# One decoder step on one core: bank matmuls issued singly, two side jobs re-timed, and the end of the program in another order

## The chip, the core and the metric

The kernel runs on one core of one Trainium2 chip. The metric is the device time of one execution in microseconds (us). The program is a single launch.

## What is computed

One inference step of a small two-layer decoder in float32, width 2048, on 1024 prompt positions and 8 single sample positions:

```
x  <- LayerNorm(ALPHA*x + (pool(x@w_in)[u] @ w_grp * scale * silu(gate)) @ w_out)   # layer A: causal pooling
k, v = shared_kv(x)                                                                # 4 heads of 64, partial rotary
x  <- LayerNorm(ALPHA*x + (attention_window128(q, k, v, sinks) * silu(gate)) @ w_out)  # layer B
LayerNorm: mean and variance over the 2048 channels, LN_EPS = 1e-5, gain g, offset b
```

Outputs are y for both kinds of positions and the new pool, key and value states.

## The kernel before

**Data and tiles.** Activations lie channel first: 128 channels on the partitions, positions along the free dimension. The positions are worked on in two chunks, c = 0 with 512 and c = 1 with 520 columns, of which a product takes half: 256 or 260. A float32 product is made of three float32r matmuls, high x high, high x low and low x high (lines 662, 663, 664), where "high" is a rounded copy (ScalarE, L491 for weights, L797 for activations) and "low" the rest (VectorE, L506 and L806).

**Seven products for eight.** Outside two plain stretches, a 2x2 block of a matrix product is made by seven products in Strassen's manner (`seven`). One of the seven, a *product* in this text, is a tile of weights with 8 x 3 = 24 matmuls into one PSUM bank. Sums of weight blocks and of activation blocks stand in DRAM for this. The banks of one block are called a, b and c. Bank b begins as the negated bank a, written there by ScalarE in `p0` (L603), and matmuls then add to it. Evictions are called p0 to p6; p6 copies the last bank (L635), p3 and p4 are subtractions on VectorE (L623, L628). An eviction is put off: it is issued at the start of the next product (`flush`, called by `begin`).

**Banks.** `psD` hands out a ring of three banks, `psW` four more where they are not used for attention scores (else the same ring), `psO` one. [...] 

**Phases.** ai (input product, pooling, gate), ao (output product) for both chunks, then bi (queries, gates, attention) and bo (output product) for both. In the order of time: ai0, ai1 (from 383 us), ao0, ao1 (from 910), bi0 plain (1075 to 1222), bi0 by sevens, bi1 (from 1508), bo0, bo1 (from 2117).

**The order of the work.** Each engine works through its instructions in the order of the source. That order comes from counters: `self.i` counts products (in the plain stretches half units), `at(n, go)` puts work n products later, and generators in `side` go on by one step at a time when `int(i / every)` changes and enough buffers are free. Two such jobs matter here:
- `sum_gen("wob")` makes the sums of the output projection's weight blocks, in 24 pieces: two loads of half a piece on SP, four adds on VectorE, a store on POOL. Pieces are begun while `on` is set, one at a time, three to four counts each. In bi0 it was set from count 4 to 24, and again in bi1 from count 8. The trace has five pieces in bi0 (1093 to 1149 us) and 19 in bi1 (1559 to 1875 us).
- `ln_gen(0, ...)` in the last phase bo1 is the first chunk's last LayerNorm: statistics, then for each of 8 pairs of tiles a load, a subtraction (L1027) and a product (L1030) on VectorE, two scalings on ScalarE (L1019) and a store.

Weights are loaded some seven products ahead on SP, split three to four ahead. A buffer is one of 54 slots; the one that was freed longest ago is taken next.

**The end** (`phase_end`). The last three blocks x, y, z = 5, 6, 7 are made in an order written out by hand (`TAIL`), and a table `steps` hangs work on each product. The second chunk's LayerNorm comes in two halves: columns 260 to 519 (Bh) get statistics early and are finished by `affine1` (two VectorE passes, L1434 and L1435) and `affine2` (two ScalarE passes, L1442, and a store). For the columns 0 to 259 (A) the statistics come after the last product: `sums_a` adds up by matmuls with a constant matrix `jr` (L1492), `moments` makes mean and reciprocal deviation in small steps between ScalarE and VectorE (L1508 to L1518, L1505), `turn` transposes the gain-scaled tiles (`scale`, L1454) on TensorE (L1537), `factors` transposes the deviation (L1526), `last_rows` adds mean and offset by matmuls (L1545), and `evict` multiplies and stores the rows (L1562 on ScalarE, L1557 on VectorE). `spare` copies the last four columns on POOL (L1457), `square` is L1403, `add` L1406 and L1407, `rest` L1398.

Of the kernel before, what the change touches and what calls it, by code (L numbers as in the profile page):

```python
# [16 lines left out]
P = 128  # L17
# [165 lines left out]
class Kern:  # L183
    def __init__(self, ctx, tc, io):
        self.tc, self.io = tc, io
        self.nc = tc.nc
        pool = lambda name, **kw: ctx.enter_context(tc.tile_pool(name=name, **kw))
        one = pool("one", bufs=1)
        self.smp = pool("smp", bufs=2)
        dram = pool("dram", bufs=1, space=bass.MemoryType.DRAM)  # L190
        self.psd = [pool(f"psd{i}", bufs=1, space=bass.MemoryType.PSUM) for i in range(3)]
        self.pso = pool("pso", bufs=1, space=bass.MemoryType.PSUM)
        self.four = None
        ctx.callback(self.use_four, None)
        self.prm = one.tile([P, N_PRM], F32, name="prm")
        self.cst = one.tile([P, N_CST], F32, name="cst")
        self.mki = one.tile([P, 64], U8, name="mki")
        self.jr = one.tile([P, P], F32R, name="jr")
        area = one.tile([P, NK * NST], F32, name="area")
        three = lambda a, b, c: area[:, a : a + b * c].rearrange("p (b c) -> p b c", b=b)  # L200
        self.carry = three(0, NK, NST)
        self.kdec, self.qd, self.sgd = three(0, 2, NDEC), three(16, NDEC, 8), three(80, 8, NDEC)
        self.flag = one.tile([P, 1], F32, name="flag")
        self.mem = Mem(pool("mem", bufs=1), NSLOT)
        self.n = 0
        self.i = self.e = self.lastO = self.turns = self.ring = 0
        self.posts, self.events, self.side = [], {}, []
        self.extra, self.on = None, False
        self.fresh = False
        self.ahead = 7, 4, 3  # L210
        dr = lambda n, s: dram.tile(s, F32, tag=n, name=n)
        self.Td, self.act, self.l_sq, self.l_sh = {}, {}, {}, {}
        for c, (_, T) in enumerate(CHUNKS):
            for n, k in (("x", "ai"), ("g", "ao"), ("h", "bi"), ("o", "bo")):
                if (k, c) in STRASSEN:
                    self.Td[n, c] = dr(f"t{n}{c}", [P, 8, 4, T // 2])
            self.act["x", c] = io[f"x{c}"]
            for n in ("g", "h", "o", "p"):
                self.act[n, c] = dr(f"{n}{c}", [P, NK, T])
        self.gbd = dram.tile([32, 2 * P], F32, tag="gbd", name="gbd")  # L220
        self.ws = {
            n: [dr(f"s{n}{q}", [P, 4, 1024]) for q in range(np_)]
            for n, np_ in (("wia", 16), ("woa", 8), ("wkv", 2), ("wib", 16), ("wob", 8))
        }
# [361 lines left out]
    def seven(self, c, z0, z1, after, c11=None, split=False, own=None):  # L586
# [13 lines left out]

        def p0():
            B["b"] = self.psD()
            nc.scalar.mul(B["b"][:, :TH], B["a"][:, :TH], -1.0)  # L603
            if split:
                nc.scalar.copy(out(0)[:, :TH], B["a"][:, :TH])
# [34 lines left out]
        def run(idx):  # L640
            bank = names[idx]
            w = self.begin()
            xs = [self.x_get((idx, g)) for g in range(2)]
            if self.fresh:

                self.fresh = False
                h = xs[0][0].rv(4, TH)[:, 0, :]
                for _ in range(3):
                    ps = self.psD()
                    nc.tensor.matmul(ps[:, :TH], w[0].r[:, :P], h, start=True, stop=True)  # L650
            new = bank not in B
            if new and own is not None and bank in "ac":
                B[bank] = own() if bank == "a" else B["a"]
            elif new:
                B[bank] = self.psW() if bank in "ac" else self.psD()
            ps = B[bank]
            wh, wl = (s.r for s in w)
            for k in range(8):
                s = slice(k * P, (k + 1) * P)
                h, l = (a.rv(4, TH)[:, k % 4, :] for a in xs[k // 4])  # L660
                on = not new
                nc.tensor.matmul(ps[:, :TH], wh[:, s], h, start=new and k == 0, stop=False, skip_group_check=on)  # L662
                nc.tensor.matmul(ps[:, :TH], wh[:, s], l, start=False, stop=False, skip_group_check=on)  # L663
                nc.tensor.matmul(ps[:, :TH], wl[:, s], h, start=False, stop=k == 7, skip_group_check=on)  # L664
            for s in w:
                s.free()
            for g in range(2):
                self.x_used((idx, g))
            self.posts.append(posts[idx])
            if idx in after:  # L670
                self.posts.append(after[idx])
            self.end()
# [695 lines left out]
    def phase_end(self, c, xs, x_in, pre, acc, gc, bc, out):  # L1368
# [116 lines left out]
        def sums_a(js):  # L1485

            z = SPLIT[-1]
            if not js:
                R[0] = self.psW(), self.psW()
            for ps, a, w in zip(R[0], (av, qv), (tv(z), self.pair_view(q[z], T))):  # L1490
                for j in js or (0, 1):
                    nc.tensor.matmul(  # L1492
                        ps[:, :TH], J, (w if js else a)[:, j, A], start=not js and j == 0, stop=js == (1,),
                        skip_group_check=True,
                    )

        def moments():

            mb, vb = R[0]
            w, h, S = self.mem.full(), self.mem.full(), [self.mem.half() for _ in range(4)]  # L1500
            m, v, qq, r = (t.a[:, :TH] for t in S)
            X, M = w.a[:, : 2 * P], h.r[:, : 2 * P]
            box["m"], box["r"], box["M"] = m, r, M
            hi, lo = slice(0, 64), slice(64, P)
            back32 = lambda k: nc.vector.tensor_sub(  # L1505
                M[k : k + 32], X[k : k + 32], h.a[k : k + 32, : 2 * P]
            )
            nc.scalar.copy(m, mb[:, :TH])  # L1508
            nc.vector.tensor_mul(qq, m, m)
            nc.scalar.mul(X[hi], mb[hi, A2], -1.0)  # L1510
            nc.vector.scalar_tensor_tensor(v, vb[:, :TH], EPS, qq, op0=ALU.add, op1=ALU.subtract)
            nc.scalar.activation(r, v, AF.Abs_reciprocal_sqrt)
            nc.scalar.copy(M[hi], X[hi])
            nc.vector.tensor_mul(qq, r, r)
            nc.vector.scalar_tensor_tensor(qq, qq, -0.5, v, op0=ALU.mult, op1=ALU.mult)
            nc.vector.scalar_tensor_tensor(r, qq, 1.5, r, op0=ALU.add, op1=ALU.mult)
            nc.vector.tensor_mul(X[lo], v[lo, A2], r[lo, A2])
            nc.scalar.copy(M[lo], X[lo])  # L1518
            back32(32)
            back32(96)  # L1520

        def factors():
# [53 lines left out]
        for p in SPLIT:  # L1576
            box, z0, z1 = self.two(T)

            def open_(p=p, box=box, z0=z0):
# [28 lines left out]
            (y, 6): [  # L1608
                lambda: add(x, A), lambda: rest(z, A), lambda: affine(y, Bh), lambda: spare(x), lambda: scale(x),
            ],  # L1610
            (z, 5): [lambda: square(y, A), lambda: affine(z, Bh), lambda: spare(4), lambda: scale(4)],
            (z, 6): [
                lambda: square(z, A, 0), lambda: add(y, A), lambda: scale(z, (0,), True),
            ],
        }
        for p, idx in TAIL:
            for go in steps.get((p, idx), []):
# [8 lines left out]
        while self.side:  # L1626
            self.side_step()
        self.flush()
        square(z, A, 1)
        spare(y)  # L1630
        spare(z)
        scale(z, (1,))
        scale(y)
        affine1(1, Bh)
        affine2(1, Bh)
        X[0, 0], X[0, 1] = self.psD(), self.psD()
        turn(0, 0, 8)
        sums_a(())
        sums_a((0,))
        sums_a((1,))  # L1640
        X[0, 2], X[0, 3] = self.psW(), self.psW()
        turn(0, 8, 16)
        X[1, 0], X[1, 1] = self.psO(), self.psD()
        turn(1, 0, 8)
        affine1(2, Bh)
        moments()
        X[1, 2] = self.psW()
        turn(1, 8, 12)
        affine2(2, Bh)
        box["c"] = self.psW()  # L1650
        factors()
        factors2()
        affine1(3, Bh)
# [5 lines left out]
        X[1, 3] = self.psD()  # L1659
        turn(1, 12, 16)  # L1660
        last_rows(1, (3,))
        affine2(3, Bh)
        affine1(4, Bh)
        for k in range(4):
            evict(1, k)
        affine2(4, Bh)
# [593 lines left out]
    def run(self):  # L2260
# [15 lines left out]
        for n, (kind, c, part) in enumerate(PHASES):  # L2276
            self.c, self.ph = c, kind + str(c)
            self.strassen = (kind, c, part) not in PLAIN
            self.shared = False
            self.fresh = c == 1 and before and self.strassen  # L2280
            before = c == 0 and self.strassen
            nxt = n + 1 if n + 1 < len(PHASES) else None
            self.every, self.room = 3, SIDE_KEEP
# [29 lines left out]
            elif (kind, c) == ("bi", 0) and not self.strassen:  # L2313
                self.summed["wob"] = 0
                self.extra = self.sum_gen("wob")
                for k in (4, 24):
                    self.at(k, lambda k=k: setattr(self, "on", k == 4))
                add(("h", 1, False), self.ln_gen(1, *acc[1], C_GA, C_BA, self.act["h", 1], self.Td.get(("h", 1))))
                for k in range(20):
                    self.at(2 * k + 3, lambda: self.side and self.lastO < self.i - 1 and self.side_step())  # L2320
# [9 lines left out]
                self.rt.free()  # L2330
            elif (kind, c) == ("bo", 1):
                gen = self.ln_gen(0, *acc[0], C_GB, C_BB, io["y0"], None)
                self.at(12, lambda gen=gen: add("y", gen))
                self.every = 1.6
            if kind == "ai":
                self.phase_ai(c, range(*part), nxt)
            elif kind == "bi":
# [155 lines left out]
```

## Time and profile before

| what | us |
|---|---|
| median of 3 runs | 2311.03 (2309.96 to 2313.41) |
| profiled execution, its own time | 2310.14 |
| its span, first to last instruction | 2308.4 |
| TensorE busy | 2283.8 |
| VectorE busy | 1905.4 |
| ScalarE busy | 1366.1 |

The span is what the profiler saw of one execution; 1.7 us of that execution's time lie around it. Engines are called PE (TensorE matmuls), PEld (its weight loads), DVE (VectorE), ACT (ScalarE), POOL and SP. A row of the timeline has the start in us from the span's start, the duration, engine, line, operation, written tile <- read tiles, shapes and count; in brackets stands how long the engine was idle before it and who ended that. Matmuls are pipelined, so the distance of two starts is what one costs, not its duration. A row "A <- B: t, n, m" of the waits says that A waited t us in n places for B, at most m in one.

### The profile page before, as it was taken

To read this page: it belongs to the slowest core of one execution; us is meant where nothing else is said; L and a number is where in the kernel's file an instruction comes from. 1 tells how busy PE (TensorE), PEld (TensorE's weight loads), DVE (VectorE), ACT (ScalarE), POOL (GpSimd) and SP (SyncE) were. 2 spreads that over 40 slices of the span, in tenths; PEclk is the share of its full clock that TensorE was granted. 3 is DMA by queue.
4 is the path that set the end of the run, shared out by engine and by line. 5 is a ranking of instruction groups with operands and counts; after the bars stand their busy time and mean duration, and the time that the engine had idled before them with its cause. 6 is when DMAs were issued, how large, how long until landed. Compare 5 with 4: busy or idle time off the path is not lost.

```text
span 2308.4 us, 50361 instructions
## 1 busy us (share of the span) xinstructions
PE 2283.8 (99%) x20258; PEld 2208.1 (96%) x20258; DVE 1905.4 (83%) x2434; ACT 1366.1 (59%) x2534; POOL 196.0 (8%) x396
## 2 busy tenths in 40 slices
PE   9999999999999999999999999999999999999997
PEld 7899999999999999999889999999999999999997
DVE  8787899777878878988978888899776777898897
ACT  4444445544546546555466776785777678646556
POOL 0111110010000000000101111100000000000001
PEclk9999999999999999999999999999999999999999
DMA  8668789988989988999777777787686768799785
GB/s 292 244 233 293 262 297 367 337 298 293 308 304 316 353 282 306 327 387 358 263 263 247 239 229 252 257 288 233 221 262 220 225 224 310 254 361 371 259 311 198
DMA packets 247978, 654.56 MB, mean 284 GB/s; under 512 B 25376, under 2 KB 106048, under 8 KB 247744
## 3 DMA queue, kind: packets, MB, share of 16 engines
q1 hardware_dynamic: 204576, 494.67, 63.8%
q0 software_dynamic: 43168, 156.68, 17.6%
q8 instruction: 158, 2.59, 0.5%
q14 instruction: 76, 0.62, 0.1%
HBM read 464.54 MB, written 177.20 MB: 278 GB/s over the span
## 4 chain that ended last, share of the span: by engine, by line
PE 53%; DVE 3%; issue 2%; DMA 1%; ACT 1%; POOL 0%; DVEq 0%; SPq 0%; POOLq 0%; ACTq 0%
PE pD L662 14%; PE pD L663 14%; PE pD L664 14%; PE pD L690 2%; PE pD L692 2%; PE pD L691 2%; PE pS L1823 2%; PE pS L1891 1%; PE pO L1930 1%; DMA m<-in_wob 1%; PE pD L1930 1%; PE pS L1930 1%; DMA m<-in_woa 0%; DVE m L506 0%; PE pO L662 0%
## 5 line engine op out<-in xcount | busy, mean ns | idle before, releaser
L662 PE MATMUL pD<-m,m 128*128 128x260 f32 (+1 forms) x4976 | 1409.1, 283 | 5.5 <-DVE m L623 2.2
L664 PE MATMUL pD<-m,m 128*128 128x260 f32 (+1 forms) x4976 | 1401.5, 282 | 0.1
L663 PE MATMUL pD<-m,m 128*128 128x260 f32 (+1 forms) x4976 | 1401.5, 282 | 0.0
L662 PEld LDWEIGHTS pD<-m,m 128*128 128x128 f32 x4976 | 936.9, 188 | 10.4 <-ACT pD L603 2.2
L664 PEld LDWEIGHTS pD<-m,m 128*128 128x128 f32 x4976 | 937.3, 188 | 0.3 <-DVE m L506 0.3
L663 PEld LDWEIGHTS pD<-m,m 128*128 128x128 f32 x4976 | 936.9, 188 | 0.5
L506 DVE TENSOR_TENSOR m<-m,m 128x1024 fp32r<-128x1024 f32 x684 | 827.8, 1219 | 77.2 <-ACT m L491 41.0
L491 ACT CAST m<-m 128x1024 fp32r<-128x1024 f32 x684 | 712.4, 1048 | 283.6 <-DVE m L343 86.8
L343 DVE TENSOR_TENSOR m<-m,m 128x1024 f32<-128x1024 f32 x120 | 146.6, 1222 | 10.0 <-DMA m<-in_wia 7.6
L806 DVE TENSOR_TENSOR m<-m,m 128x1024 fp32r<-128x1024 f32 (+1 forms) x118 | 144.2, 1225 | 7.6 <-ACT m L797 4.9
L635 ACT COPY m<-pD 128x260 f32<-128x260 f32 (+1 forms) x87 | 32.5, 374 | 191.5 <-PE pD L664 191.5
L797 ACT CAST m<-m 128x1024 fp32r<-128x1024 f32 (+1 forms) x118 | 123.6, 1052 | 4.3 <-DMA m<-in_x 2.5
L690 PE MATMUL pD<-m,m 128*128 128x512 f32 x288 | 114.3, 397 | 0.0
L692 PE MATMUL pD<-m,m 128*128 128x512 f32 x288 | 113.5, 394 | 0.0
L691 PE MATMUL pD<-m,m 128*128 128x512 f32 x288 | 113.3, 393 | 0.0
L623 DVE TENSOR_TENSOR m<-pD,m 128x260 f32<-128x260 f32 (+1 forms) x90 | 38.1, 423 | 74.7 <-PE pD L664 74.7
L1864 ACT ACTIVATE m<-m,sm 128x128 f32<-128x128 f32 x256 | 99.2, 390 | 0.0
L1886 ACT ACTIVATE m<-m,sm 128x128 f32<-128x128 f32 (+1 forms) x320 | 93.7, 372 | 0.0
L1134 PE MATMUL pD<-m,m 128*128 128x260 f32 (+1 forms) x528 | 91.4, 323 | 0.0
L1134 PEld LDWEIGHTS pD<-m,m 128*128 128x128 f32 x528 | 79.4, 188 | 8.2
L612 ACT COPY m<-pD 128x260 f32<-128x260 f32 (+1 forms) x90 | 33.7, 374 | 90.0 <-PE pD L664 89.7
L603 ACT ACTIVATE pD<-pD 128x260 f32<-128x260 f32 (+1 forms) x88 | 32.4, 369 | 81.6 <-PE pD L664 81.2
(258 smaller groups left out, 2183.8 us busy)
## 6 DMA issues: line engine op xcount, KB each, us to landing
m<-in_wib SPq DMA_DIRECT2D x132, 512.0 KB
m<-in_wia SPq DMA_DIRECT2D x122, 512.0 KB
swia<-m POOLq DMA_DIRECT2D x64, 512.0 KB, 4.9
m<-swia SPq DMA_DIRECT2D x64, 512.0 KB
m<-swoa SPq DMA_DIRECT2D x64, 512.0 KB
m<-swob SPq DMA_DIRECT2D x56, 512.0 KB
m<-in_wob SPq DMA_DIRECT2D x52, 512.0 KB
m<-in_woa SPq DMA_DIRECT2D x48, 512.0 KB
```

Of the source, the lines that this page charges most:

```text
L343: self.nc.vector.tensor_add(s[out].a[:, :1024], s[x].a[:, :1024], s[y].a[:, :1024])
L491: self.nc.scalar.copy(hi.r[:, :1024], self.stream[self.cast].src().a[:, :1024])
L506: self.nc.vector.tensor_sub(lo.r[:, :1024], s.src().a[:, :1024], hi.a[:, :1024])
L662: nc.tensor.matmul(ps[:, :TH], wh[:, s], h, start=new and k == 0, stop=False, skip_group_check=on)
L663: nc.tensor.matmul(ps[:, :TH], wh[:, s], l, start=False, stop=False, skip_group_check=on)
L664: nc.tensor.matmul(ps[:, :TH], wl[:, s], h, start=False, stop=k == 7, skip_group_check=on)
L690: nc.tensor.matmul(ps[:], wh[:, s], h, start=par == 0 and k == 0, stop=False)
L691: nc.tensor.matmul(ps[:], wh[:, s], l, start=False, stop=False)
L692: nc.tensor.matmul(ps[:], wl[:, s], h, start=False, stop=par == 1 and k == 7)
L797: self.nc.scalar.copy(h.r[:, :n], s.a[:, :n])
L806: self.nc.vector.tensor_sub(l.r[:, :n], s.a[:, :n], h.a[:, :n])
L1134: nc.tensor.matmul(ps[:, : cs.stop - cs.start], ws[:, s], d[:, cs], start=f0 and k == 0, stop=l0 and k == 3,)
```

## The change

Bank matmuls: the three at the start of a phase go; in their place `p0` issues one for each ring bank, the first time that the phase takes it as bank b, with the constant `jr` as weights and a resident activation tile as data. Weight sums: `on` is set from count 20 to 38 of bi0 instead of 4 to 24. Norm: the side job of bo1 starts at product 11 instead of 12 and goes on every 1.25 instead of 1.6 products. End: y's and z's work on `steps` is moved, all of z's statistics squares come in one, the sums come directly after them, `affine(z)` comes after the last product, `affine1(2)` and `affine2(1)` come after `moments`, `affine2(2)` behind the first evictions. In `moments` the negated mean is made from the copy in SBUF instead of from PSUM, and two small steps are exchanged. Five matmuls of 512 columns go into the bank of the factors ahead of them; nothing reads what they write.

```diff
-        self.fresh = False
+        self.fresh = None
...
         def p0():
             B["b"] = self.psD()
+            if self.fresh is not None and self.ring not in self.fresh:
+                self.fresh.add(self.ring)
+                nc.tensor.matmul(
+                    B["b"][:, :TH], self.jr[:], self.X[0, 0][0].rv(4, TH)[:, 0, :], start=True, stop=True
+                )
             nc.scalar.mul(B["b"][:, :TH], B["a"][:, :TH], -1.0)
...
-            if self.fresh:
-                self.fresh = False
-                h = xs[0][0].rv(4, TH)[:, 0, :]
-                for _ in range(3):
-                    ps = self.psD()
-                    nc.tensor.matmul(ps[:, :TH], w[0].r[:, :P], h, start=True, stop=True)
...
             nc.vector.tensor_mul(qq, m, m)
-            nc.scalar.mul(X[hi], mb[hi, A2], -1.0)
             nc.vector.scalar_tensor_tensor(v, vb[:, :TH], EPS, qq, op0=ALU.add, op1=ALU.subtract)
+            nc.scalar.mul(X[hi], m[hi, A2], -1.0)
+            nc.scalar.copy(M[hi], X[hi])
             nc.scalar.activation(r, v, AF.Abs_reciprocal_sqrt)
-            nc.scalar.copy(M[hi], X[hi])
+            back32(32)
...
             nc.scalar.copy(M[lo], X[lo])
-            back32(32)
             back32(96)
...
-            (z, 5): [lambda: square(y, A), lambda: affine(z, Bh), lambda: spare(4), lambda: scale(4)],
-            (z, 6): [
-                lambda: square(z, A, 0), lambda: add(y, A), lambda: scale(z, (0,), True),
-            ],
+            (z, 5): [lambda: square(y, A), lambda: spare(4), lambda: scale(4)],
+            (z, 6): [lambda: add(y, A), lambda: spare(y), lambda: scale(y)],
...
-        square(z, A, 1)
-        spare(y)
+        square(z, A)
+        sums_a(False)
+        sums_a(True)
+        X[0, 0], X[0, 1] = self.psD(), self.psD()
         spare(z)
-        scale(z, (1,))
-        scale(y)
+        scale(z, (0, 1), True)
+        affine1(z, Bh)
+        affine2(z, Bh)
         affine1(1, Bh)
-        affine2(1, Bh)
-        X[0, 0], X[0, 1] = self.psD(), self.psD()
         turn(0, 0, 8)
-        sums_a(())
-        sums_a((0,))
-        sums_a((1,))
         X[0, 2], X[0, 3] = self.psW(), self.psW()
         turn(0, 8, 16)
         X[1, 0], X[1, 1] = self.psO(), self.psD()
         turn(1, 0, 8)
-        affine1(2, Bh)
         moments()
+        affine2(1, Bh)
         X[1, 2] = self.psW()
         turn(1, 8, 12)
-        affine2(2, Bh)
+        affine1(2, Bh)
         box["c"] = self.psW()
+        for _ in range(5):
+            nc.tensor.matmul(box["c"][:], self.jr[:], box["g", 0].r[:, :512], start=True, stop=True)
         factors()
...
         last_rows(1, (3,))
+        affine1(4, Bh)
+        affine2(2, Bh)
         affine2(3, Bh)
-        affine1(4, Bh)
...
-            self.fresh = c == 1 and before and self.strassen
+            self.fresh = set() if c == 1 and before and self.strassen else None
...
-                for k in (4, 24):
-                    self.at(k, lambda k=k: setattr(self, "on", k == 4))
+                for k in (20, 38):
+                    self.at(k, lambda k=k: setattr(self, "on", k == 20))
...
-                self.at(12, lambda gen=gen: add("y", gen))
-                self.every = 1.6
+                self.at(11, lambda gen=gen: add("y", gen))
+                self.every = 1.25
```

More of the change, by code (lines that the diff above doesn't have):

```diff
@@ L1490, in sums_a @@
             for ps, a, w in zip(R[0], (av, qv), (tv(z), self.pair_view(q[z], T))):
-                for j in js or (0, 1):
+                for j in range(2):
                     nc.tensor.matmul(
-                        ps[:, :TH], J, (w if js else a)[:, j, A], start=not js and j == 0, stop=js == (1,),
+                        ps[:, :TH], J, (w if js else a)[:, j, A], start=not js and j == 0, stop=js and j == 1,
                         skip_group_check=True,
```

## The prediction

> **What bounds the kernel now.** I read the page's busy times first, then TensorE's waits, then the timelines at the places where TensorE waits, the windows of DMA and VectorE beside them, and last the chain that ended last.
>
> ```profile
> span 2308.4 us, 50361 instructions
> PE 2283.8 (99%) x20258; PEld 2208.1 (96%) x20258; DVE 1905.4 (83%) x2434; ACT 1366.1 (59%) x2534; POOL 196.0 (8%) x396
> PE pD L650 <- ACT m L635: 4.2, 3, 2.4
> PE pD L1526 <- DVE m L1516: 1.9, 1, 1.9
> ```
>
> TensorE is busy for all but 24.6 us, so an edit can gain only where TensorE stands still, or behind its last product. The third line (total, times, longest) is the largest wait of all: the bank matmuls at L650 wait 4.2 us in three places for ScalarE's copy at L635. The places, and what the other engines did there:
>
> ```profile
> 910.35 0.40 PE L650 MATMUL pD<-m,m 128*128 128x260 f32 x2
> 913.14 0.39 PE L650 MATMUL pD<-m,m 128*128 128x260 f32 x1 [2.40 <-ACT m L635]
> ...
> 1508.36 0.28 PE L650 MATMUL pD<-m,m 128*128 128x260 f32 x1
> 1508.99 0.51 PE L650 MATMUL pD<-m,m 128*128 128x260 f32 x2 [0.34 <-ACT m L635]
> ...
> 2116.72 0.40 PE L650 MATMUL pD<-m,m 128*128 128x260 f32 x2
> 2118.62 0.39 PE L650 MATMUL pD<-m,m 128*128 128x260 f32 x1 [1.50 <-ACT m L635]
> ...
> 930.80 0.28 PE L663 MATMUL pD<-m,m 128*128 128x260 f32 x1
> 930.92 0.29 PE L664 MATMUL pD<-m,m 128*128 128x260 f32 x1
> ...
> 913.12 1.22 DVE L1288 SCALAR_TENSOR_TENSOR m<-m,m 128x1024 f32<-128x1024 f32 x1 [1.83 <-ACT m L635]
> 928.03 1.22 DVE L506 TENSOR_TENSOR m<-m,m 128x1024 fp32r<-128x1024 f32 x1
> 2119.74 1.22 DVE L506 TENSOR_TENSOR m<-m,m 128x1024 fp32r<-128x1024 f32 x1
> 2124.83 0.28 PE L664 MATMUL pD<-m,m 128*128 128x260 f32 x1
> ```
>
> Matmuls of 260 columns start 0.12 us apart (930.80, 930.92); 24 of them, one product, are 2.88 us.
>
> **The change, part by part.** *Bank matmuls singly.* Three matmuls at the start of the four second-chunk phases go; one is put ahead of the first use of each of the three ring banks as bank "b". The old three ask for all three banks at once, also the one that the last product of the phase before has just filled. The new first one is issued a product later (2.88 us) and takes the next bank of the ring, the one longest out of use; in the third phase, where pairs use the ring three at a time, it takes the filled one, but 2.88 us after the copy could start, against 0.63 us that the old wait took. So I expect no wait there. Worked out per place:
> - 910: the third matmul would have started at 910.59 and started at 913.14: 2.55 us stood still. How much of it stays gained is set by VectorE: from L1288 at 913.12, which waits for the same ScalarE copy, it runs without a gap, and the L506 of 928.03 makes, by count, the low half that TensorE first uses at 930.92. It ends at 929.25, so 1.67 us is all that TensorE can move ahead of it. Ends 0.5 and 2.55; I take 1.67, since that order of VectorE isn't changed.
> - 1508: 0.63 between two starts less 0.12, and one matmul fewer, since only two banks of the ring serve as "b" there: 0.63. Ends 0 and 0.9.
> - 2116: the third would have started at 2116.96, started at 2118.62: 1.66. The low half made at 2119.74 is ready at 2120.96 and used at 2124.83: 3.87 in hand, so all of it stays. Ends 0.8 and 1.66.
> - The first phase has no wait in TensorE's list: 0. ScalarE's negated copy behind each new matmul starts at most 0.12 us later, where a product of 2.88 us covers it.
>
> *Weight sums later, denser norm.* Nothing is added, 24 pieces (two loads on SP, four VectorE adds, one store on POOL each) and 16 norm steps move.
>
> ```profile
> 980.00:1000.00 20.00, 20.00 (x169) 20.00 (x168) 19.62 (x27) 13.49 (x19) 2.13 (x4) 1.00 1.01 392
> 1136.00:1203.00 67.00, 67.00 (x428) 53.96 (x427) 54.43 (x85) 48.23 (x103) 6.10 (x13) 1.00 0.79 278
> 2180.00:2210.00 30.00, 30.00 (x253) 30.00 (x252) 29.69 (x30) 19.76 (x28) 1.08 (x2) 1.00 0.91 311
> 2210.00:2240.00 30.00, 30.00 (x253) 30.00 (x252) 27.21 (x27) 17.74 (x27) 1.58 (x2) 1.00 0.93 336
> ...
> L1030 DVE TENSOR_TENSOR m<-m,m 128x1024 f32<-128x1024 f32 x8 | 9.7, 1216 | 0.0
> ...
> 1239.54 2.35 DVE L806 TENSOR_TENSOR m<-m,m 128x1024 fp32r<-128x1024 f32 x2
> 1242.37 0.36 PE L662 MATMUL pD<-m,m 128*128 128x256 f32 x1 [1.16 <-DVE m L623]
> ```
>
> Windows read: length, busy TensorE, weight load, VectorE, ScalarE, POOL, clock, DMA share, GB/s. The sums' first pieces (five) leave a stretch without TensorE waits for one of 67 us without any either (1136 to 1203), with a fifth of the DMA time and VectorE 12 us free: cost 0. Without that cover five pieces of 1 MB cost 13 us at 392 GB/s. The norm's 16 VectorE steps, 1.2 us each (L1030; another line has eight as well), come every 1.25 instead of 1.6 products: in 30 us some 8.3 for 6.5, 2.2 us more work where VectorE was busy 29.69 and 27.21 and DMA 0.91. The rows above show weights ready 1.67 and 3.87 us ahead of their use, and that lead absorbs the 2.2: cost 0, ends 0 and 3. On SP the norm's loads and stores stand in one queue with the weight loads, and a store that waits for ScalarE holds these back as now, only closer together; the same lead covers it. What the edit brings: the norm's some 24 steps from product 11 on, one in 1.25, end at product 41 of 56, not at 51, so none is left in the last ten.
>
> *The end.* Chain of waits (start, us, what), then SP and windows:
>
> ```profile
> 2285.07 1.41 ACT m L1019 x2
> 2286.48 0.53 ACT m L1403
> 2287.01 0.99 ACT m L1442 x2
> 2288.00 0.80 ACT m L1454 x2
> ...
> 2289.82 1.20 ACT m L1454 x3
> 2291.02 0.99 ACT m L1442 x2
> 2292.01 0.27 ACT m L1508
> ...
> 2296.49 0.71 DVE m L1434
> ...
> 2297.84 1.40 DVE m L1557 x2
> ...
> 2302.16 0.66 DVE m L1557
> ```
>
> ```profile
> 2285.01 1.04 PE L1537 MATMUL pD<-cst,m 128*128 128x128 f32 x8
> 2303.31 0.57 SPq L1443 DMA_DIRECT2D out_y<-m  x1
> 2298.00:2300.00 2.00, 2.00 (x8) 1.60 (x7) 1.90 (x6) 2.00 (x5) 0.00 (x0) 0.50 0.65 244
> 2300.00:2302.00 2.00, 0.50 (x2) 0.00 (x0) 1.97 (x4) 1.29 (x3) 0.00 (x0) 0.81 1.02 401
> 2304.00:2306.00 2.00, 0.00 (x0) 0.00 (x0) 0.00 (x0) 0.00 (x0) 0.00 (x0) 0.54 0.99 379
> ```
>
> ScalarE works without a pause from 2285.07 to 2292.01 (6.94 us) before it copies the mean at L1508, and all later steps hang on that. In the new order its queue between the same points is: square(y) 0.53, scale(4) 0.80, scale(y) 0.80, square(z) 0.53, scale(z) 0.80, affine2(z) 0.99: 4.45. Gone are the norm's L1019 (1.41), affine2(1) (0.99, now behind the statistics) and a split square. That is 2.5 us; the norm's missing VectorE step ahead lets the queue start some 0.6 sooner: 3.1. Ends 2.4, and 4.2 (last product at 2285.01, then copy and square 0.9, 0.80, 0.99). Behind the statistics stand now two VectorE passes of affine1(2), 1.35 (L1434 to L1557), ahead of the first eviction: the evictions end 3.1 - 1.35 = 1.75 sooner. But the end is not theirs: DMA is full from 2300 to 2306. Four stores of 512 KB and two halves of 260 KB follow the first eviction; now it is three halves: 0.27 MB at some 390 GB/s is 0.7 us. So the end gains 1.05. Ends 0.3 and 2.2.
>
> The five matmuls and the reordered statistics lines: TensorE stands still 1.9 us there (L1526), and five of 512 columns at twice the 260-column pace are 1.2: cost 0; 0.3 if they start late. The clock had fallen to 0.50 at 2298, and the last matmul's bank waits for VectorE anyway: 0 from the clock too. [...]
>
> [...]
>
> **Sum.** 1.67 + 0.63 + 1.66 + 1.05 = 5.0 us. The profiled execution took 2310.14 us (1.7 about the span), 0.9 below the median of the runs, 2311.03. So 2305.1 for a like execution, 2306.0 for the median. About 0.2% (4.6 us, to 2306.4) is what a measurement of this kernel tells from no change.
>
> **The rivals.**
> - *The denser norm takes some back.* VectorE is at 29.69 of 30 us and gets 2.2 more: 1.9 don't fit, and with weight loads late behind a DMA share of 0.91 TensorE would wait 2.3 us: 2308.3. It decides where the lead in weights is below 2. Against it: the next 30 us have 2.8 free.
> - *The waits come back.* The bank matmul waits where it stands, or VectorE and DMA (full at 980 to 1000) don't follow a TensorE that is 1.67 ahead. Without the three gains of 4.0: 2310.0; with half of them 2308.
> - *The end gains more.* Norm over early, mean copied 4.2 sooner, and 910 gains 2.55: 2304.0.
> - *Slower: the late sums reach the next phase.* Their 13 us of DMA time, in the 14 that 1136 to 1203 has free, delay the reads that L806 splits. At 1239.54 VectorE makes the last two of these, to 1241.89, for a product that starts at 1242.37 and already waits 1.16. A delay above 0.5 us goes into TensorE's time at once; all 13 would give 2318. It turns the sum to slower from 9.6 on. Against it: DMA share is 0.79 over that stretch, and 36 us lie between.
>
> **How the numbers follow.** Forecast 0.50, its own range 2304.5 to 2307.4 (some three quarters of the ends at 910 and in the tail), of which 0.36 lies below 2306.4; the end gains more 0.14; norm 0.14 and waits back 0.15, both within 0.2%; slower 0.07. So faster 0.50, same 0.43, slower 0.07. The range leaves out the slower case and the outer parts of the others: 2303.0 to 2310.0.
>
> **What would show it.** Right: no wait of a bank matmul in TensorE's list; TensorE ahead by 1.7 at 960, by 4.0 at 2200; the product at 930.92's place waiting little for L506; no L1019 after 2260's place; L1508 7 us earlier on the clock of the span, the last L1557 5.7, the end 5.0; DMA still full for 6 us or more. Wrong: new waits on L506 between 2150 and 2250, a longer wait than 1.16 at the 1242 place, or an end that follows the evictions alone.

## The result, and the profile after

The changed kernel takes 2307.10 us (median of 13 runs, 2305.69 to 2309.54), the kernel before in the same comparison 2312.04 (13 runs, 2308.85 to 2314.56): ratio 0.9977, 95% interval 0.9970 to 0.9985, 4.9 us by the medians. Forecast was 2306.0 against 2311.03, a ratio of 0.9978. The profiled execution took 2306.19, 3.95 less than that of before. That the sum of 5.0 is met by the medians and not by this pair of traces turns out to matter.

The page of the changed kernel, span, busy times, and TensorE's waits (total, times, longest):

```profile
span 2304.4 us, 50373 instructions
PE 2282.2 (99%) x20262; PEld 2208.2 (96%) x20262; DVE 1904.9 (83%) x2434; ACT 1365.9 (59%) x2533; POOL 197.2 (9%) x396
...
PE pD L661 <- DVE m L629: 2.3, 2, 1.3
PE pD L661 <- ACT pD L609: 1.8, 2, 1.3
PE pD L661 <- ACT m L618: 1.5, 1, 1.5
...
PE pD L663 <- DVE m L506: 1.1, 1, 1.1
```

No wait of a bank matmul is left (it stands at L606 now). Lines moved by one or more: L661 to L663 are the product's three matmuls, L629 is p3, L609 the copy behind the bank matmul. Two waits that weren't there have come: one of 1.12 us for the low half of a weight tile at L506, and one of 1.26 us for the eviction p3 at 2175 us. The list has two waits for p3 because one has gone, that of 1.16 us at 1242. The list of before had two as well:

```profile
PE pD L662 <- DVE m L623: 2.2, 2, 1.2
```

The timeline of the changed kernel at these places, TensorE first:

```profile
910.21 0.28 PE L661 MATMUL pD<-m,m 128*128 128x260 f32 x1
929.38 0.39 PE L663 MATMUL pD<-m,m 128*128 128x260 f32 x1 [1.12 <-DVE m L506]
935.72 0.50 PE L910 MATMUL pO<-m,jr 128*128 128x512 f32 x1 [0.35 <-DVE m L894]
2117.41 0.29 PE L606 MATMUL pD<-m,jr 128*128 128x260 f32 x1
2117.53 0.28 PE L661 MATMUL pD<-m,m 128*128 128x260 f32 x1
2175.24 0.36 PE L661 MATMUL pD<-m,m 128*128 128x260 f32 x1 [1.26 <-DVE m L629]
...
928.12 1.21 DVE L506 TENSOR_TENSOR m<-m,m 128x1024 fp32r<-128x1024 f32 x1
934.98 1.28 DVE L894 TENSOR_TENSOR m<-m,m 128x512 fp32r<-128x512 f32 x2
2171.18 1.23 DVE L1341 TENSOR_TENSOR m<-m,m 128x1040 f32<-128x1040 f32 x1
2172.61 0.69 DVE L932 TENSOR_TENSOR m<-m 128x512 f32<-128x512 f32 x1 [0.20 <-ACT m L931]
2173.34 0.69 DVE L933 SCALAR_TENSOR_TENSOR m<-m 128x512 f32<-128x512 f32 x1
2174.06 0.69 DVE L934 SCALAR_TENSOR_TENSOR m<-m,m 128x512 f32<-128x512 f32 x1
2174.67 0.42 DVE L629 TENSOR_TENSOR m<-pD,m 128x260 f32<-128x260 f32 x1
```

At 2117.41 the bank matmul and the next matmul start 0.12 us after what precedes them. At 928 VectorE's L506 starts 0.1 later than before (928.03), and TensorE, now early, stands 1.12 us for it. At 2172 the denser norm's three deviation passes lie between L1341 and the eviction p3, and TensorE waits 1.26 for that.

I call *lead* how much earlier a product starts than the same one before (both from their span's start), worked out from the starts of the 630 products in the two traces (the plain stretches are left out). Where it changes:

| place | forecast | trace | why |
|---|---|---|---|
| up to 910 | 0 | +0.15 | there before 383 already; three bank matmuls fewer at 383 give 0.36, the single ones behind them take it back |
| 910 to 960 | +1.67 | +0.53 | +3.01 at 910 (2.65 of it without the three bank matmuls themselves), then -0.33 (two single ones and small steps), -1.39 (L506 at 929), -0.61 (L894 at 935), -0.17 (the third single one and a small step) |
| 960 to 1242 | 0 | +0.33 | small steps |
| 1242 to 1508 | 0 | +0.74 | +1.09 (the wait of 1.16 is 0.09), then -0.35 in small steps |
| 1508 | +0.63 | +0.40 | +1.00, then -0.60 |
| to 2116 | 0 | +0.06 | |
| 2116 | +1.66 | +1.87 | +2.11, then -0.13, and small steps |
| 2120 to the last product | 0 | -1.50 | the new wait of 1.26 at 2175, the third single bank matmul, small steps |
| behind the last product | +1.05 | +1.38 | below |

The end of the changed kernel, from the chain of waits (start, us, what), and its windows (length, busy TensorE, weight load, VectorE, ScalarE, POOL, clock, DMA share, GB/s):

```profile
2284.09 0.53 ACT m L1402
2284.61 0.80 ACT m L1453 x2
2285.41 0.99 ACT m L1441 x2
2286.41 0.27 ACT m L1507
...
2293.59 1.40 DVE m L1556 x2
...
2297.91 0.66 DVE m L1556
```

```profile
2296.00:2298.00 2.00, 0.00 (x0) 0.00 (x0) 1.97 (x4) 0.72 (x2) 0.00 (x0) 0.79 1.02 397
2298.00:2300.00 2.00, 0.00 (x0) 0.00 (x0) 0.57 (x1) 0.38 (x1) 0.00 (x0) 0.50 1.01 375
2300.00:2302.00 2.00, 0.00 (x0) 0.00 (x0) 0.00 (x0) 0.00 (x0) 0.00 (x0) 0.50 0.99 379
```

The mean copy (L1507, L1508 before) comes 5.60 us earlier and the last eviction 4.25 (2302.16 before). Counted from the start of the last product's last matmul (2284.89 before, 2282.32 now), the copy comes after 3.98 us instead of 7.02, the last eviction ends after 16.24 instead of 17.93, and the program after 22.10 instead of 23.48: 3.04, 1.69 and 1.38 gained, against 3.1, 1.75 and 1.05 in the forecast. DMA is full for six us, from 2296 to 2302, as it was from 2300 to 2306.

### The profile page after: what moved, and what is told of

It is laid out like the page before. It is cut to its first block, busy times and chain, and to the rows that moved or that the text cites. A ratio compares the mean times of both kernels' runs of the same rounds, so it can differ in the third digit from the quotient of the medians.

```text
span 2304.4 us, 50373 instructions
## 1 busy us (share of the span) xinstructions
PE 2282.2 (99%) x20262; PEld 2208.2 (96%) x20262; DVE 1904.9 (83%) x2434; ACT 1365.9 (59%) x2533; POOL 197.2 (9%) x396
## 5 line engine op out<-in xcount | busy, mean ns | idle before, releaser
L661 PE MATMUL pD<-m,m 128*128 128x260 f32 (+1 forms) x4976 | 1409.0, 283 | 5.6 <-DVE m L629 2.3
L663 PE MATMUL pD<-m,m 128*128 128x260 f32 (+1 forms) x4976 | 1401.3, 282 | 1.2 <-DVE m L506 1.1
L661 PEld LDWEIGHTS pD<-m,m 128*128 128x128 f32 x4976 | 936.8, 188 | 10.8 <-issue 2.3
L663 PEld LDWEIGHTS pD<-m,m 128*128 128x128 f32 x4976 | 937.3, 188 | 1.7 <-DVE m L506 1.7
L506 DVE TENSOR_TENSOR m<-m,m 128x1024 fp32r<-128x1024 f32 x684 | 827.7, 1218 | 73.8 <-ACT m L491 38.5
L629 DVE TENSOR_TENSOR m<-pD,m 128x260 f32<-128x260 f32 (+1 forms) x90 | 38.1, 423 | 74.2 <-PE pD L663 74.2
L609 ACT ACTIVATE pD<-pD 128x260 f32<-128x260 f32 (+1 forms) x88 | 32.5, 369 | 78.6 <-PE pD L663 67.8
```

The lines of the kernel that those rows point to most:

```text
L506: self.nc.vector.tensor_sub(lo.r[:, :1024], s.src().a[:, :1024], hi.a[:, :1024])
```

## Experiments

Theory: the bank waits make most of the gain, what VectorE and DMA let stay of it; the norm gives at the end and takes at 2175. Rivals: the gain is the end's or the sums', or the traces' difference is chance. All ratios are to the kernel before on the same chip.

**Each part alone in the kernel before.** Single bank matmuls (e1_banks), late sums (e2_sums), denser norm (e3_norm), new end with the five matmuls (e4_end):

```diff
 e1:  bank matmuls in p0 instead of three at L650 (first two hunks of the change)
 e2: -for k in (4, 24):                  +for k in (20, 38):
 e3: -self.at(12, ...add("y", gen))      +self.at(11, ...add("y", gen))
     -self.every = 1.6                   +self.every = 1.25
 e4:  the hunks in steps, moments and phase_end
```

> The kernel before with the bank matmuls issued singly and nothing else. Theory of the prediction: the three waits go and stay gone, 1.67 + 0.63 + 1.66 = 4.0 us less. Theory from the two traces: TensorE gains 2.6, 0.6 to 1.0 and 1.7 at the three phase starts, but about 2.0 of the first is given back within eight products, at the first use of a low half that VectorE made too late (1.4) and at a sum matmul that waits for VectorE (0.6); so some 2.5 us less at the last product, and the wait of 1.16 at the start of the second part of phase bi0 stays as it was. Rival: the single matmuls wait themselves, 0 to 1 us less.

> The kernel before with only the weight sums of phase bi0 set from count 20 to 38. Theory of the prediction: no change, 0 us, since neither stretch has a wait of TensorE. Theory from the two traces: the wait of 1.16 us for VectorE's eviction near 1242 us shrinks to about 0.1, because VectorE is no longer held up by 2.5 us at 1230 for a buffer that is still being stored: 1.1 us less. Rival: that wait goes by the earlier arrival of TensorE or by other buffers, not by the sums; then it stays here.

> The kernel before with only the last phase's norm started at product 11 and stepped every 1.25 products. Theory of the prediction: no loss in the phase, and the end starts earlier, since the 1.41 us of the norm's scalings ahead of the last squares go: 1 to 2 us less, as far as the stores at the end allow. Theory from the two traces: a new wait of 1.3 us for VectorE's eviction near 2176 us, behind three steps of the norm's deviation, eats most of that: 0 to 0.5 us less. Rival: DMA or VectorE fall behind over the whole stretch, 2 us more.

> The kernel before with only the new order of the end and the five matmuls; the norm still ends late. Theory of the prediction: the norm's 1.41 us stay in ScalarE's queue, so the copy of the mean comes 4.45 + 1.41 after 2285.07 and not 6.94, 1.1 sooner; 1.35 more of VectorE and 0.27 MB more of stores behind it: 0 to 1 us more than before. Rival: the order alone makes the gain of 1.4 that the two traces show behind the last product, and the norm adds nothing to it.

| alone | median us (before 2311.72) | ratio | end behind the last matmul's start |
|---|---|---|---|
| banks | 2310.47 | 0.9992 (0.9983 to 1.0000) | 23.84 |
| sums | 2310.93 | 0.9997 (0.9988 to 1.0006) | 23.62 |
| norm | 2311.39 | 0.9997 (0.9989 to 1.0006) | 21.41 |
| end | 2313.00 | 1.0007 (0.9997 to 1.0016) | 23.94 |

The banks alone show the changed kernel's pattern at 910 (+3.01, then -1.11 and -0.62 at the same two places), 1508 and 2116; their lead grows by 2.3 in all, and the second theory had 2.5. With the late sums alone the wait at 1242 stays, 1.0 us: there the rival was right. The norm alone brings the wait at 2175 (1.2 us) and the whole gain at the end, 2.07; the new order alone makes the end 0.46 longer. The norm came as its second theory had it; the order, 1.3 us slower by the medians, is a little over its theory's 0 to 1. Summed, the four ratios give 0.0007, the whole gives 0.0023. Four intervals of about 0.0009 each make some 0.0018, so the gap may be chance; an interplay is possible too (see the sums at 1242 and the granted clock, below).

**The whole without one part.** Without the denser norm (a1_no_norm), without the five matmuls (a2_no_five), with the norm of ao1 begun later (a3_h_norm_late), with the old end (a5_old_end), without the single bank matmuls (a6_no_banks):

```diff
 a1: -self.at(11, ...) / self.every = 1.25          +self.at(12, ...) / self.every = 1.6
 a2: -for _ in range(5):
     -    nc.tensor.matmul(box["c"][:], self.jr[:], box["g", 0].r[:, :512], ...)
 a3: -self.at(3, ...add(("h", 0, True), gen))       +self.at(8, ...add(("h", 0, True), gen))
 a5:  steps, moments and phase_end as before, no five matmuls
 a6:  three matmuls at L650 as before, p0 without
```

> The changed kernel with the last phase's norm as before (product 12, every 1.6). Theory: the wait of 1.3 us near 2175 us is the denser norm's and goes here, but the end loses 1.8 (23.9 after the last product instead of 22.1): 0.4 us slower than the changed kernel, about 4.5 less than before. Rival: the wait near 2175 comes from TensorE's earlier arrival and stays; then 1.8 slower than the changed kernel.

> The changed kernel without the five matmuls in the bank of the factors. Theory: VectorE and the stores set the end, so nothing changes, 0 us, even if the clock falls a few us sooner and the last rows take twice as long. Rival: the five keep the clock up for the last rows, and without them the end is 0.5 to 1.9 us later.

> The changed kernel with the norm in phase ao1 started at product 8 instead of 3. Theory: what TensorE gave back after 910 us (1.4 for a late low half, 0.6 for a sum matmul of that norm) comes from two VectorE sums of that norm in the first six products, where VectorE works without a gap; moved behind them, 1.5 to 2 us less than the changed kernel, about 6.5 less than before. Rival: VectorE is full there anyway and TensorE waits elsewhere before 1000 us: no change.

> The changed kernel with the end in its old order and without the five matmuls; bank matmuls, sums and norm as changed. Theory: the end's gain is the norm's, not the order's. With the norm early and the old order the program ended 21.41 us after its last product, with both 22.10, so this one should be 0.7 us faster than the changed kernel: about 5.5 us less than before. Rival: the new order pays once the norm is gone, and this one is 1 us slower than the changed kernel.

> The changed kernel with the old three bank matmuls put back in each of the three stages: the weight sums, the denser norm and the new end stay. Theory (the banks carry most of the change, the norm's other place and the end the rest): TensorE waits 2.0 to 2.4 us again at 910, 1.0 at 1508 and 1.5 to 2.1 at 2116, the waits of 0.8 to 1.1 at 929 do not appear, the one of 1.2 to 1.3 at 2175 does, the end behind the last product is 22.1 long; the span is 2307.3 to 2308.5 in an execution whose stores land as early as in the changed kernel, and the ratio to the kernel before is 0.9988 to 0.9996, so the banks are worth 0.0012 to 0.0020 in the whole. Rival (the banks' gain is given back entirely, and the change is faster for its norm and end): ratio 0.9975 to 0.9983, the same as the changed kernel's. If the granted clock halves behind the wait at 910 for one record of 3.4 us, the profile shows 1.4 us more.

| the change | median us | before | ratio | end behind the last matmul's start |
|---|---|---|---|---|
| whole | 2307.10 | 2312.04 | 0.9977 (0.9970 to 0.9985) | 22.10 |
| without denser norm | 2308.05 | 2311.69 | 0.9984 (0.9975 to 0.9992) | 23.94 |
| without five matmuls | 2307.58 | 2311.69 | 0.9976 (0.9967 to 0.9986) | 22.18 |
| ao1's norm later | 2308.00 | 2311.69 | 0.9987 (0.9978 to 0.9996) | 22.06 |
| old end | 2305.74 | 2311.69 | 0.9973 (0.9963 to 0.9983) | 21.64 |
| without single banks | 2309.63 | 2311.38 | 0.9997 (0.9988 to 1.0006) | 22.25 |

Without the single bank matmuls the gain is gone: they are worth 0.0020 in the whole, 4.6 us, give or take 2.7 (both intervals combined). The norm's 0.0007 lies inside its uncertainty; its trace without it has no wait between 2120 and 2270 and an end 1.84 longer, so it gives 1.84 and takes some 1.5. The five matmuls are worth nothing that shows, as their theory had it. The new order of the end costs 0.46 us of end in two pairs (before to end alone; old end to whole) and 0.69 in a third (norm alone, 21.41, to whole), and no run shows it to help. It does bring the mean copy forward: counted from the last matmul's start the copy comes after 7.02 us before, 5.94 with the new order alone, 5.02 with the norm alone and 3.98 with both. But the last store of the program is issued after 18.42, 18.67, 16.41 and 16.73.

a3 asks what took the gain at 910 back. Its theory, 1.5 to 2 us faster than the changed kernel, did not come true: the ratio is 0.9987 against 0.9977. With ao1's norm begun five products later neither 929 nor 935 has a wait and the lead grows to 4.24 at 943, some 0.9 of it matmuls of that norm which come later now. But waits come 100 and 130 us later (0.4 and 0.9 us, at 1038 and 1065); a3's VectorE at that place, and its windows, with those of the changed kernel below:

```profile
1064.41 1.23 DVE L506 TENSOR_TENSOR m<-m,m 128x1024 fp32r<-128x1024 f32 x1 [2.51 <-DMA p<-m]
...
1010.00:1075.00 65.00, 63.66 (x525) 63.11 (x524) 56.13 (x68) 38.55 (x52) 4.92 (x11) 1.00 1.01 393
```

```profile
1010.00:1075.00 65.00, 65.00 (x544) 64.96 (x543) 50.65 (x58) 35.05 (x48) 3.86 (x9) 1.00 0.97 365
```

With the norm moved there, DMA has more to do (393 GB/s for 365). L506 waits 2.51 us for a buffer that a store of the phase's own sums (tile `p`, L1294) still reads; in the changed kernel, without such a wait there, that store takes 5.3 us from issue to landing. TensorE waits for L506, and at 1134 the lead is 1.41, against 0.90 in the changed kernel; as a3 had 0.48 ahead of 910 already, and the changed kernel 0.15, that is 0.2 us kept. So this move doesn't keep the gain of 910: what VectorE no longer takes at 929 is lost to a store at 1064. Other places for the norm weren't tried.

**Three tries at a faster kernel**, all with the old end: stored operands' buffers given out again after 20 releases instead of 10 (b1_release20), the last norm begun a product later at the same pace (b2_norm12), both (b3_both).

```diff
 b1: -s.free(True)                        +self.mem.release(s, 20)          # in t_ops
 b2: -self.at(11, ...add("y", gen))       +self.at(12, ...add("y", gen))    # every 1.25
```

> The changed kernel with the old end (0.9973 of the time before), and the buffers that hold a stored operand given out again twenty releases later instead of ten. Theory (where VectorE's weight part at 1230 waits for a buffer that a store still reads, 1.4 us in the profile with the old end, TensorE is late by 0 to 3 us at 1242, by how long the store takes in that execution): VectorE waits for no store near 1230, TensorE waits under 0.3 us at 1242 in every execution, and the median falls by 0.3 to 1.0 us, ratio 0.9968 to 0.9972. Rival (the buffer that is taken in its place is still in use by something else, or the late store was hidden in most executions): ratio 0.9971 to 0.9980, and a new wait of VectorE or of a load stands near 1230.

> The changed kernel with the old end, and the last product stage's denser norm begun one product later (product 12, steps still every 1.25 products). Theory (TensorE's wait of 1.27 us at 2175 comes only from the three deviation passes of 0.7 us lying ahead of the eviction that it waits for; one product later they lie behind it): that wait falls under 0.4 us, the last product ends 0.5 to 1.0 sooner against product 628, the end behind it is 21.6 to 22.2 long, ratio 0.9969 to 0.9973. Rival (VectorE has no room anywhere between 2165 and 2180): the wait moves by one or two products with the same 0.9 to 1.3 us, ratio 0.9973 to 0.9977. The norm ending a product later could also lengthen the end: it was 23.9 long with the norm from product 12 at every 1.6.

> The changed kernel with the old end, the stored buffers given out again twenty releases later, and the last norm begun at product 12 with steps every 1.25. Theory: both effects add, no wait of TensorE above 0.4 us at 1242 and 2175, ratio 0.9963 to 0.9970, the fastest of all. Rival: the later release shifts other buffers so that one of them is taken while still read, and the ratio stays at 0.9971 to 0.9978.

b1 took 2308.91, ratio 0.9991 (0.9982 to 1.0000): the rival's side, and above even the rival's range. VectorE near 1230 with the old end, and with the later release:

```profile
1228.64 1.23 DVE L506 TENSOR_TENSOR m<-m,m 128x1024 fp32r<-128x1024 f32 x1 [1.43 <-DMA to<-m]
```

```profile
1232.31 1.23 DVE L805 TENSOR_TENSOR m<-m,m 128x1024 fp32r<-128x1024 f32 x1 [2.01 <-issue]
```

The wait for the store is gone from L506; the activation's low half two passes later waits 2.01 us for something the profile doesn't name, and TensorE waits 1.2 us at 1242. It also waits 1.16 us at 2132, on ScalarE's L624, where it had waited 0.2. b3 has the same wait of 2.0 near 1230: 2308.09, ratio 0.9986 (0.9978 to 0.9995), so both effects together gave nothing of what was expected.

b2 took 2305.73, ratio 0.9977 (0.9967 to 0.9986), profiled span 2302.2, the shortest here. Its wait for p3 in TensorE's list:

```profile
PE pD L661 <- DVE m L629: 1.1, 1, 1.1
```

One place where the changed kernel has two: 2175 is gone, and the lead from 2124 to the last product falls by 0.04 instead of 1.5. The end is 22.04 instead of 21.64. In the traces that is 1.0 us better than the old end with product 11, if this one loses the same 1.5; its own trace loses 1.97 there. So the theory held in the trace, but the ratio is in the rival's range (0.9973 to 0.9977), and the ratios don't separate the two kernels. Both have medians 1.4 us under the changed kernel's, but in other comparisons, and their intervals contain its ratio: no version here is shown to beat it.

## Why the forecast held, point by point

**No wait of a bank matmul: right.** It rests on all three places and the run without them, and it is the main cause of the gain: without them 0.0020 of the 0.0023 is gone. Alone they gave 0.0008 (0.0000 to 0.0017), and the leads at their places add up to 2.8 us, so how much of the 0.0020 needs the other parts as well stays open. Every kernel here has bank matmuls, three at the start of a phase or one for each ring bank, so the runs show what they cost in time and not what they are for.

**910: the term was mis-sized, 1.67 against 0.53.** The step that failed is "1.67 us is all that TensorE can move ahead of it", taken as gain. The bound itself was good: TensorE's matmul that needs L506 started at 929.38, 1.54 ahead of 930.92, and one product on the lead was 1.43. But it is a bound on the clock of the span, and 0.15 of that lead was there before 910. And the next bound, VectorE's L894 for the statistics matmuls at 935, was not looked for. It took 0.61 more, and the third single bank matmul with a small step 0.17. "TensorE ahead by 1.7 at 960" was 0.7.

**1508 and 2116: about right.** 0.40 kept for 0.63, 1.9 for 1.66. "So all of it stays" held at 2116: no weight was late behind it, as the 3.87 us in hand promised.

**The norm at cost 0: wrong, -1.5.** The forecast asked whether weights would be late. They weren't; VectorE's evictions were. Three passes of 0.69 in front of a p3 that TensorE waits for made 1.26 us. They belong to the norm's statistics; the forecast's 16 steps of 1.2 us left them out. The rival "the denser norm takes some back" had the size (up to 2.3), by another way. The "new waits on L506 between 2150 and 2250" did not come. The lead at 2200, forecast as 4.0, was 2.5, and with it the copy came 5.6 us earlier, not 7, and the last eviction 4.25, not 5.7.

**The end: the sizes about right, one conclusion missed.** 3.04, 1.69 and 1.38 against 3.1, 1.75 and 1.05. That the stores set the last part held. The forecast's list of what is gone mixes the norm's part (1.41 for L1019 and 0.6 for its VectorE step, 2.0) and the order's (the remaining 1.1, less 1.35 for the two VectorE passes and 0.7 for the third half store: a loss of some 0.95). Alone, the norm brought the copy 2.00 sooner and the end 2.07; the order brought the copy 1.08 sooner and made the end 0.46 longer. So the terms were near, and by these terms the new order doesn't pay, which the forecast didn't say.

**The sums at cost 0: no loss, perhaps a gain.** The slower rival, late sums reaching 1242, did not show in the times, and in the changed kernel's trace the wait there was 0.09. (It isn't always: without the five matmuls, with the same sums, it was 2.5, behind a store that took 9.4 us.) Between 1205 and 1235 DMA moved 7.96 to 8.00 MB in the six profiles that have single banks and late sums with the old release, and 8.45 to 8.68 in the six that lack one or both. TensorE's wait at 1242 is 0.6 us on average in the first (0, 0, 0.1, 0.3, 0.8, 2.5), 1.5 in the second (0.9, 1.0, 1.1, 1.2, 1.9, 3.1). The spread is as large as the difference, so some 0.9 us from the two together is possible and not settled. It would be an interplay that neither part alone shows.

**The five matmuls and the clock: right, 0.** The end is 22.18 without them and 22.10 with them; the 0.5 to 1.9 us that a2's rival gives them for keeping the clock up did not come.

**The sum: in part luck.** 910 gave 1.14 less than forecast and the norm took 1.50 that was not in the sum. Leads that the sum didn't have (0.15, 0.33, 0.74 and 0.06, most of it from the wait at 1242) gave 1.28 of this back, and the end 0.33. So the traces make 3.95 for 5.0, by misses that partly cancel, and the medians' 4.9, with an interval of some 1.7 us to either side, is nearer to the forecast than its terms were.

**Chance in the pair of traces.** The terms of the traces make 3.95, the medians 4.9. One part of the difference is named below: behind the wait at 910 the clock was 0.50 for 3.41 us in three of five profiles, and that of before happened not to be one of them. Other waits come and go as well: five of the 14 profiles, but neither of this pair, have one of TensorE of 1.0 to 1.2 us near 1690; with the old end VectorE waited 1.8 us for a DMA there.

## What the runs showed of the hardware

**Behind four waits of 2.0 to 3.0 us the granted clock was 0.50 for 3.41 us, behind others it stayed at 1.00.** At the end of the trace of before the granted clock changes at 2297.34, 2300.76 and 2304.17 us, 3.41 us apart each time. Windows of that length around a wait at 910: of the kernel with late sums alone (a wait of 2.29 us), of the one without single banks (3.0), and of the kernel before (2.40; these lie 405 to 407 such lengths ahead of 2297.34).

```profile
910.94:914.35 3.41, 1.33 (x11) 1.34 (x12) 1.68 (x3) 3.41 (x5) 0.00 (x0) 1.00 1.07 384
914.35:917.77 3.42, 3.42 (x19) 3.42 (x18) 3.42 (x4) 0.52 (x1) 0.54 (x1) 0.50 1.05 383
```

```profile
910.86:914.27 3.41, 0.94 (x7) 0.94 (x8) 1.00 (x2) 3.26 (x5) 0.00 (x0) 1.00 1.06 382
914.27:917.68 3.41, 3.41 (x18) 3.41 (x17) 3.41 (x4) 0.93 (x1) 0.33 (x1) 0.50 1.04 381
```

```profile
908.12:911.53 3.41, 2.63 (x23) 2.42 (x21) 3.18 (x4) 1.28 (x2) 0.00 (x0) 1.00 1.05 387
911.53:914.94 3.41, 1.79 (x14) 1.80 (x15) 1.81 (x2) 3.41 (x5) 0.00 (x0) 1.00 1.06 386
914.94:918.35 3.41, 3.41 (x31) 3.41 (x30) 3.41 (x4) 1.93 (x4) 0.54 (x1) 1.00 1.05 386
```

The first number behind the length is TensorE's busy time. With 1.33 and 0.94 us in a window the next had a clock of 0.50 and 19 or 18 matmuls where before's has 31. Before's wait of 2.40 falls across two windows, neither goes below 1.79, and the clock stays at 1.00. The kernel with the new end alone has the longest wait of all, 3.14 us at 1242:

```profile
1238.85:1242.26 3.41, 1.85 (x16) 1.65 (x14) 3.41 (x4) 2.27 (x9) 0.53 (x1) 1.00 0.00 0
1242.26:1245.68 3.42, 1.84 (x15) 1.87 (x16) 3.42 (x4) 2.92 (x12) 0.00 (x0) 1.00 0.39 158
1245.68:1249.09 3.41, 3.41 (x32) 3.41 (x31) 3.34 (x7) 1.78 (x3) 1.07 (x2) 1.00 0.44 173
```

Split evenly over two windows, 1.85 and 1.84 us of work, it left the clock at 1.00. Of the windows read around such waits ahead of the end, the four with 0.94, 0.95, 1.33 and 1.36 us of TensorE work were followed by a clock of 0.50 (0.95 without the five matmuls, from 1239.03, a wait of 2.46; 1.36 with the norm alone, from 909.01, a wait of 2.05), those with 1.57 (norm alone, from 1240.10), 1.79, 1.84, 1.85 and 2.63 by one of 1.00. What decides it, no run shows. The drop cost 1.5 us in the kernel without single banks (lead from -0.19 to -1.69). Of the five profiles that have the wait at 910 (2.0 to 3.0 us) three have the drop; in the six others that were read there, from 905 to 925, the clock is 1.00. So the wait costs some 0.9 us more on average than its own length, an estimate from these counts and the 1.5. It fits the 4.9 against 3.95, though with one profile for each kernel it isn't shown to be the whole of it.

The executions that weren't profiled say more, as each one's mean granted clock is on record. It is 0.9971 on average over 96 executions of the kernel before, where the profiled one, without such a drop, had 0.998, and 0.9984 over the 13 of the changed kernel. The six kernels with single banks, late sums and the old release have 0.9982 to 0.9985, those that lack one or both 0.9971 to 0.9980. One window of 3.41 us at half clock takes 0.0007 from this mean, over a span of 2308 us. So an execution of the kernel before has some 1.8 such windows more than one of the changed kernel, 2.7 us at 1.5 each. That is an estimate, and an upper one: windows behind the last product count in the mean, and need not cost time. The kernel without single banks has 0.9980, half a window more than the changed kernel. Where the rest of the windows falls no trace shows; with early sums, the wait at 1242 is a candidate.

**How long a store was in flight moved whole waits.** The kernels before, with the norm alone and with the end alone have the same source code up to the last phase. The store that VectorE waits for near 1230 took 8.1, 8.8 and 10.1 us in them from issue to landing, and TensorE's wait at 1242 went from 1.16 to 1.9 and 3.14 us with it. The changed kernel and the one without the five matmuls, again alike up to there, have 6.8 and 9.4 us, with waits of 0.09 and 2.46. The rows of the kernel before and of the end alone (512 KB, us to landing):

```profile
to<-m POOLq DMA_DIRECT2D x1, 512.0 KB, 8.1
```

```profile
to<-m POOLq DMA_DIRECT2D x1, 512.0 KB, 10.1
```

## What to carry to other kernels

A stall that is removed is worth what the next bound leaves: take that bound on the clock of the span, subtract the lead that is there already, and look one bound further, as 0.61 us went to the second one here. Before side work is made denser, check not only the loads but which evictions its passes will stand in front of. And behind some TensorE waits of 2.0 to 3.0 us the clock was 0.50 here for 3.41 us, a second price of some 1.5 us that one profile need not show: compare several executions before a trace's difference is taken for the effect.
